# A hybrid attention and recurrent step: the recurrent unit's last tiles and the projections behind them in another order

## The chip, the cores and the metric

One core of a Trainium2 chip. The metric is the device time of one execution in microseconds (us), the median over runs of the same kernel. The engines are TensorE (PE, with its weight loads PEld), VectorE (DVE), ScalarE (ACT), GpSimd (POOL) and SyncE (SP, which here only issues DMAs).

## What is computed

Two layers of a hybrid trunk on 640 tokens (512 latent, 128 prompt) with 1024 features. Layer 0 mixes tokens by attention, layer 1 by a bidirectional gated linear recurrent unit; each is followed by a SwiGLU feed-forward network. The part around the change is the end of the attention and the recurrent unit with its output projection:

```python
def _lru_mixer(xm, h0, w_in, conv_w, conv_b, w_a, b_a, w_i, b_i, lam, w_out):
    gate, xr = jnp.split(xm @ w_in, 2, axis=-1)
    xc = _centred_depthwise_conv(xr, conv_w, conv_b).astype(jnp.float32)
    a_f, b_f = _rglru_coeffs(xc, w_a[0], b_a[0], w_i[0], b_i[0], lam[0])
    a_b, b_b = _rglru_coeffs(xc, w_a[1], b_a[1], w_i[1], b_i[1], lam[1])
    hs_f, hT_f = _linear_scan(a_f, b_f, h0[:, 0], reverse=False)
    hs_b, hT_b = _linear_scan(a_b, b_b, h0[:, 1], reverse=True)
    y = (hs_f + hs_b).astype(xm.dtype) * jax.nn.gelu(gate)
    return y @ w_out, jnp.stack([hT_f, hT_b], axis=1)
```

`_rglru_coeffs` holds two sigmoids, an exponential and a square root for each direction.

## The kernel before

Activations lie transposed: features on the 128 partitions, in 8 tiles of 128 features (k or f = 0..7), tokens in the free dimension. All matrix products run in a 32-bit format with the inputs split in two: a high part that is the cast of the value, and a low part that is the value minus the high part. `split` (L1331) makes both, the cast on ACT (L1333) and the subtraction on DVE (L1335). For each k a product takes three matmuls (`some`, L227 to L229): high weights by high input, high weights by low input, low weights by high input, all into one PSUM buffer. Groups of a unit of 128 output features cover the 640 tokens in two halves of 320 (in the recurrent unit 384 and 256).

The weights of such a unit are loaded by `unit`: the raw tile by SP, and the high part either by a cast on ACT (L180) or, in the recurrent unit, by a DMA that POOL issues (L178); the low part is DVE's (L182). High and low tiles have three buffers each in the names `whi` and `wlo`; a slot "x" has tiles of its own, `whx` and `wlx`. Plain PSUM groups have the name `mm` with three buffers; in the last stage three more are named `mx`.

The order of the instructions is set by a scheduler that plays the program through on a timeline, so code that moves shifts other work as well. `pin` makes one instruction wait for another in that order.

Attention works through 8 head pairs p. For the next pair, `qk` casts Q and K into high parts (QS, KS, on ACT) and subtracts for the low ones (KZ for K, on DVE), for two heads a = 0, 1. The call for pair 7 is made inside pair 6. Behind it, the attention's output O of pairs 0 to 6 is split into `ohi` and `olo`, pinned behind the K operations (`parted`), since the output projection of k=0..6 fills PE between the softmax steps of pair 7. Softmax goes by blocks: scores `sp` (L831, L832), operations on DVE and ACT into S, transposes `tp` (L849), and products with V `op` (L932). Pair 7's O is split last.

The recurrent unit runs over t, with tile f of each step one later than that of the step ahead: projection `lru_xr`, gate matmuls and tanh `lru_a` (L1291, L1292), coefficients `lru_b` (exponentials L1303, L1304; a square root L1305; two operations on DVE, L1306 and L1307), scans `lru_c` (L1316, the sums of both directions L1323 and L1324), the GELU branch `lru_gate` and the product `lru_d` (L1328) with the split of y into `yhi` and `ylo`. ACT holds one function table at a time, and `turn` (L1266) loads another (L1270) when a function of another table is due: exponentials with tanh, square root, gelu. `lru_gate` copies the first 384 tokens of a gate from PSUM (L1343) and takes the gelu of the last 256 straight from PSUM (L1346), which keeps that PSUM buffer until the table is there.

The projection behind it (`project_halves`) has 8 output units. Five groups start early, while y is not yet complete: units 0 and 1 in both halves and unit 2 in the first half. They go through k=0..5 group by group, then through k=6 and 7 group by group, each with its three matmuls per k; in between stand some matmuls that compute nothing needed (`keep`, L206). Then follow the other units, whose k all exist.

Of the kernel before, what the change touches and what calls it, by code (L numbers as in the profile page):

```python
# [125 lines left out]
class _Step:  # L126
# [33 lines left out]
        return self.t([P, KT, NTOK + 2], dt, "big", 4)[:, :, 0:n]  # L160


    def unit(self, src, slot=None, after=None):
        nc = self.nc
        _, a, b = src.shape
        raw = self.t([P, a, b], F32, "raw", 3)
        nc.sync.dma_start(raw, src)
        if slot is None:
            self.nu += 1
            slot = "x" if self.wx and self.nu % 2 == 0 else "m"  # L170
        if slot == "x":
            hi = self.t([P, a, b], F32R, "whx", 3, self.sb)
            lo = self.t([P, a, b], F32R, "wlx", 3, self.sb)
        else:
            hi = self.t([P, a, b], F32R, "whi", 3)
            lo = self.t([P, a, b], F32R, "wlo", 3)
        if self.ptags == ["at"]:
            nc.gpsimd.dma_start(hi, src)  # L178
        else:
            nc.scalar.copy(hi, raw)  # L180
        with self.tc.issue_after(after) if after else nullcontext():
            nc.vector.tensor_tensor(lo, raw, hi.bitcast(F32), ALU.subtract)  # L182
        return hi, lo
# [601 lines left out]
                nc.vector.tensor_copy(K[:, 832:960], ps[:, 192:320])  # L785
        return K, ek

    def qk(self, p, hi, lo, ap, Q=None, K=None):
# [12 lines left out]
        pairs = [(QS, Q, [Q, Q]), (KS, K, [KZ[:, 0], KZ[:, 1]])]  # L801
        for S, v, lo in pairs if p else pairs[::-1]:
            for a in range(2):
                hp = slice(a * HD, a * HD + HD)
                op = slice(HD - a * HD, P - a * HD)
                cast = nc.scalar.copy(S[hp, a], v[hp]).ins
                low = nc.vector.tensor_tensor(lo[a][hp], v[hp], S[hp, a].bitcast(F32), ALU.subtract).ins
                queue = nc.gpsimd if p in (0, 7) else nc.sync
                queue.dma_start(S[op, a].bitcast(F32), Q[hp] if v is Q else S[hp, a].bitcast(F32))
        self.parted = low, cast  # L810
        return QS, KS, KZ

    def vq(self, q, hi, lo, V):
# [214 lines left out]
    def project_halves(self, w, hi, lo, gk, key, xd):  # L1028
        def out(f, t0, t1, ps):
            self.residual(f, t0, t1, ps, G, True)  # L1030
            self.nc.sync.dma_start(xd[f * P:f * P + P, t0:t1], self.x[:, f, t0:t1])
        G = self.need(self.gcols, gk)
        us = [self.unit(w[f], "m") for f in range(3)]
        early = [(f, t0, t1) for f in range(3) for c, (t0, t1) in enumerate(CH) if c == 0 or f < KT - DEH]
        pss = [(self.ps("mx") if j % 2 else self.pg(False))[:, 0:HT] for j in range(len(early))]
        for ks in (range(KT - 2), range(KT - 2, KT)):
            if ks[0]:
                self.keep(self.ps("at"), 4)
            for (f, t0, t1), ps in zip(early, pss):
                self.some(us[f], hi, lo, t0, t1, ps, ks)  # L1040
                if ks[0]:
                    out(f, t0, t1, ps)
        for f in range(3, KT):
            us.append(self.unit(w[f], "mx"[f % 2]))
            out(f, *CH[0], self.chunk(us[f], hi, lo, *CH[0]))
        self.rt = self.t([P, NTOK], F32, "r", 2)
        for c, (t0, t1) in enumerate(CH):
            for f in range(KT - DEH, KT) if c else ():
                out(f, t0, t1, self.chunk(us[f], hi, lo, t0, t1))
                j = f - KT + DEH  # L1050
                for k in range(max(0, 2 * j - 2), 2 * j) if f < KT - 1 else ():
# [195 lines left out]
        c = CI["ba0"] * KT  # L1247
        nc.vector.tensor_scalar(self.hb, self.cols[:, c:c + 4 * KT], 0.5, None, ALU.mult)

    def halves(self, w, hi, lo, ev, after=None):  # L1250
        u = self.unit(w, None, after)
        return [lambda t0=t0, t1=t1, **kw: ev(t0, self.chunk(u, hi, lo, t0, t1, **kw)) for t0, t1 in CHL]

    def lru_xr(self, f, hi, lo, after=None):
# [70 lines left out]
        return y  # L1325

    def lru_d(self, f, y, G, yhi, ylo):
        self.nc.vector.tensor_tensor(y, y, G, ALU.mult)  # L1328
        self.split(yhi[:, f], ylo[:, f], y)

    def split(self, hi, lo, v, after=(None, None)):  # L1331
        with self.pin(after[1]):
# [4 lines left out]
    def lru_gate(self, f, hi, lo, lp, after=None):  # L1337
        nc = self.nc
        G = self.t([P, NTOK], F32, "gl", 3, lp)

        def ev(t0, ps):
            if t0 == 0:
                nc.scalar.copy(G[:, 0:384], ps)  # L1343
                return
            for v, o in ((ps, G[:, t0:NTOK]), (G[:, 0:t0], G[:, 0:t0])):
                self.turn(AF.Gelu_apprx_tanh, lambda: nc.scalar.activation(o, v, AF.Gelu_apprx_tanh))  # L1346
        return G, self.halves(self.i["wi"][f], hi, lo, ev, after)

    def new_x(self, st):
        pool = st.enter_context(self.tc.tile_pool(name="x", bufs=1, reuse_waits="tile"))  # L1350
# [6 lines left out]
    def run(self):  # L1357
# [35 lines left out]
        with self.phase("attn", tp=2, sp=2, op=1, quota=24) as ap:  # L1393
# [10 lines left out]
            for p in range(8):  # L1404
                if p == 3:
                    with self.pin(self.anchor):
                        self.lru_prep(ap)
                new = []
                self.attend(p, *QK, V, O, ap, (lambda: new.extend(self.qk(7, xhi, xlo, ap))) if p == 6 else None)
                if p == 5:  # L1410
                    self.need(self.AB, (0, 1, 1))
                if p < 7:
                    QK = new or self.qk(p + 1, xhi, xlo, ap, None if p else Q1)
                    if p % 2 == 1:
                        self.vq((p + 1) // 2, xhi, xlo, V)
                if p == 6:
                    ohi = self.big()
                    olo = self.big()
                    for k in range(KT - 1):
# [22 lines left out]
        with self.phase("lru", at=1) as lp:  # L1442
# [15 lines left out]
            for t in range(KT + 2):  # L1458
# [6 lines left out]
                    B[t - 1] = self.lru_b(t - 1, *A.pop(t - 1))  # L1465
                if t > 1:
                    C[t - 2] = self.lru_c(t - 2, *B.pop(t - 2))
                if t > 2:
                    for step in gate(t - 2):
                        step()  # L1470
                if t > 1:
                    self.lru_d(t - 2, C.pop(t - 2), G.pop(t - 2), yhi, ylo)
# [35 lines left out]
```

## Time and profile before

| what | before |
|---|---|
| time, median of 3 runs | 1517.01 us (1516.26 to 1520.28) |
| time of the profiled execution | 1518.63 us |
| its span in the profile | 1516.9 us |
| mean granted clock of TensorE | 0.996 |
| PE busy | 1490.0 us (98%) |
| DVE busy | 1063.5 us (70%) |
| ACT busy | 702.6 us (46%) |
| POOL busy | 260.6 us (17%) |

A row of a timeline gives the start, the duration of one instruction (or the length of a run of equal ones, xcount), the engine, the line, the operation, output and inputs, and in brackets the idle time of the engine just before it with the instruction that ended it. Matmuls overlap, so their rate is read from the distances of the starts. A row of the windows gives for each engine the busy time, then the granted clock, the share of the DMA engines and GB/s.

### The profile page before, as it was taken

How to read it: one execution, taken by the hardware profiler on the slowest of the kernel's cores; microseconds unless marked ns; L12 is line 12 of the kernel's file. 1: busy time of each engine (PE TensorE's matmuls, PEld its weight loads, DVE VectorE, ACT ScalarE, POOL GpSimd, SP SyncE). 2: the span in 40 equal slices, each digit the busy share in tenths (PEclk: the TensorE clock that was granted, in tenths of full speed). 3: DMA queues.
4: the chain of work that ended last, by engine and by line, in shares of the span. 5: the costliest groups of instructions: out<-in, count | busy, mean ns of one | idle time of the engine just before them, and what ended most of it. 6: DMA issues, size and time to landing. Idle time of an engine off the chain costs nothing. (4 is left out here: it accounts for less than half of the span.)

```text
span 1516.9 us, 26173 instructions
## 1 busy us (share of the span) xinstructions
PE 1490.0 (98%) x10397; PEld 1443.2 (95%) x10397; DVE 1063.5 (70%) x2005; ACT 702.6 (46%) x1270; POOL 260.6 (17%) x276
## 2 busy tenths in 40 slices
PE   8999999999999999999999999989999999999997
PEld 6999999899999999999999988889999999999997
DVE  5778998679999997434443768886975665566555
ACT  4676766654332123312321568884644342434243
POOL 0112132101111110000000014230332323222211
PEclk9999999999999999999999999999999999999999
DMA  9544665446566664222222544325242231323211
GB/s 376 175 142 159 187 190 168 118 141 193 180 182 196 206 197 132 62 84 84 65 69 87 153 133 128 105 68 198 70 152 84 70 112 56 104 64 98 70 57 70
DMA packets 72330, 196.65 MB, mean 130 GB/s; under 512 B 8048, under 2 KB 24592, under 8 KB 72080
## 3 DMA queue, kind: packets, MB, share of 16 engines
q1 hardware_dynamic: 57392, 142.32, 29.7%
q0 software_dynamic: 14240, 51.98, 11.3%
q8 instruction: 81, 1.33, 0.4%
q10 hardware_dynamic: 576, 0.68, 0.1%
q14 instruction: 41, 0.34, 0.1%
HBM read 179.48 MB, written 8.92 MB: 124 GB/s over the span
## 5 line engine op out<-in xcount | busy, mean ns | idle before, releaser
L227 PE MATMUL mm<-big,whi 128*128 128x320 f32 (+3 forms) x1233 | 385.4, 314 | 5.7 <-ACT gl L1346 3.0
L228 PE MATMUL mm<-big,whi 128*128 128x320 f32 (+3 forms) x1233 | 384.8, 312 | 4.9 <-DVE big L1335 4.7
L229 PE MATMUL mm<-big,wlo 128*128 128x320 f32 (+3 forms) x1233 | 383.5, 312 | 0.0
L227 PEld LDWEIGHTS mm<-big,whi 128*128 128x128 f32 x1233 | 233.7, 190 | 8.6 <-ACT gl L1346 3.5
L228 PEld LDWEIGHTS mm<-big,whi 128*128 128x128 f32 x1233 | 234.1, 190 | 6.9 <-DVE big L1335 5.3
L229 PEld LDWEIGHTS mm<-big,wlo 128*128 128x128 f32 x1233 | 233.6, 190 | 1.0
L256 DVE SCALAR_TENSOR_TENSOR mprod<-mraw,csb 128x1024 f32<-128x1024 f32 x160 | 195.6, 1222 | 11.9 <-DMA mraw<-in_wm 11.4
L597 DVE SCALAR_TENSOR_TENSOR x<-mm,G,x 128x320 f32<-128x320 f32 (+2 forms) x192 | 78.0, 435 | 81.8 <-PE mm L229 81.5
L180 ACT CAST whi<-raw 128x1024 fp32r<-128x1024 f32 (+1 forms) x71 | 73.9, 1041 | 112.5 <-PE mm L228 65.5
L182 DVE TENSOR_TENSOR wlo<-raw,whi 128x1024 fp32r<-128x1024 f32 (+1 forms) x87 | 105.8, 1216 | 27.4 <-ACT whi L180 11.4
L227 PE MATMUL mm<-big,whx 128*128 128x320 f32 (+3 forms) x348 | 108.3, 311 | 0.0
L229 PE MATMUL mm<-big,wlx 128*128 128x320 f32 (+3 forms) x348 | 108.0, 310 | 0.0
L228 PE MATMUL mm<-big,whx 128*128 128x320 f32 (+3 forms) x348 | 107.8, 310 | 0.0
L252 POOL DMA_DIRECT2D mraw<-in_wm x80 | 43.1, 539 | 359.0 <-DVE mprod L256 266.1
L227 PE MATMUL mx<-big,whi 128*128 128x320 f32 (+3 forms) x287 | 89.1, 311 | 0.0
L229 PE MATMUL mx<-big,wlo 128*128 128x320 f32 (+3 forms) x287 | 88.8, 310 | 0.0
L228 PE MATMUL mx<-big,whi 128*128 128x320 f32 (+3 forms) x287 | 88.6, 309 | 0.0
L180 ACT CAST whx<-raw 128x1024 fp32r<-128x1024 f32 (+1 forms) x40 | 41.1, 1030 | 86.7 <-PE mm L228 47.6
L227 PE MATMUL mx<-big,whx 128*128 128x320 f32 (+3 forms) x260 | 80.6, 310 | 0.0
L229 PE MATMUL mx<-big,wlx 128*128 128x320 f32 (+3 forms) x260 | 80.5, 310 | 0.0
L228 PE MATMUL mx<-big,whx 128*128 128x320 f32 (+3 forms) x260 | 80.3, 309 | 0.0
L1333 ACT CAST whi<-raw 128x1024 fp32r<-128x1024 f32 (+1 forms) x41 | 41.3, 1008 | 70.8 <-PE mm L228 44.8
(349 smaller groups left out, 3727.8 us busy)
## 6 DMA issues: line engine op xcount, KB each, us to landing
raw<-in_gu SPq DMA_DIRECT2D x88, 512.0 KB, 3.5
mraw<-in_wm POOLq DMA_DIRECT2D x80, 512.0 KB, 4.0
raw<-in_dn SPq DMA_DIRECT2D x24, 512.0 KB, 3.6
sw<-in_wm SPq DMA_DIRECT2D x16, 512.0 KB, 10.5
raw<-in_wqk SPq DMA_DIRECT2D x16, 512.0 KB, 4.6
raw<-in_wi SPq DMA_DIRECT2D x16, 512.0 KB, 3.5
whi<-in_wi POOLq DMA_DIRECT2D x16, 512.0 KB, 4.0
raw<-in_dn SPq DMA_DIRECT2D x16, 448.0 KB, 3.3
```

Of the source, the lines that this page charges most:

```text
L180: nc.scalar.copy(hi, raw)
L182: nc.vector.tensor_tensor(lo, raw, hi.bitcast(F32), ALU.subtract)
L227: nc.tensor.matmul(ps, hi[:, k], xhi[:, k, s], start=(k == 0), stop=False)
L228: nc.tensor.matmul(ps, hi[:, k], xlo[:, k, s], start=False, stop=False)
L229: self.done = nc.tensor.matmul(ps, lo[:, k], xhi[:, k, s], start=False, stop=(k == last)).ins
L252: nc.gpsimd.dma_start(w, self.i["wm"][l * 6 + j - 2, f])
L256: nc.vector.scalar_tensor_tensor(prod, w, 1.0, self.csb[:, s], ALU.mult, ALU.mult, accum_out=out[:, s, f:f + 1])
L597: self.nc.vector.scalar_tensor_tensor(xs, ps[:, a - t0:b - t0], G[:, s, f:f + 1], xs, ALU.mult, ALU.add)
L1333: self.nc.scalar.copy(hi, v)
```

## The change

Four things change.

1. `project_halves`: the five early groups go through k=0..4 group by group. Then k=5, 6 and 7 have a pass each: within a pass, over all five groups sorted by token half, first both matmuls with the high input (high and low weights), then for all groups the one with the low input. The keep-alive matmuls stand ahead of k=7 only.
2. The recurrent unit's last tiles: gates 5 and 6 have their gelus in one step (t=7), under one load of the table, and gate 7 comes a step earlier (t=8). Gate 7's second half is copied from PSUM like the first, and one gelu of 640 works in place. For tile 7 the product and the split go in two halves of 320.
3. The weights of gates 6 and 7 go into `whx` and `wlx`, two buffers each, so `whi` and `wlo` are free sooner for the projection's first units.
4. At the end of attention, the split of O[0] is issued between the K casts of pair 7: the cast (L815 after) behind the first K cast, the low part (L817 after) behind the first KZ operation.

```diff
-    def unit(self, src, slot=None, after=None):
+    def unit(self, src, slot=None, after=None, nx=3):
...
-            hi = self.t([P, a, b], F32R, "whx", 3, self.sb)
-            lo = self.t([P, a, b], F32R, "wlx", 3, self.sb)
+            hi = self.t([P, a, b], F32R, "whx", nx, self.sb)
+            lo = self.t([P, a, b], F32R, "wlx", nx, self.sb)
...
-                cast = nc.scalar.copy(S[hp, a], v[hp]).ins
+                with self.pin(self.opened if a and S is KS and p == 7 else None):
+                    cast = nc.scalar.copy(S[hp, a], v[hp]).ins
...
-        self.parted = low, cast
+                self.parted = low, cast
+                if p == 7 and S is KS and a == 0:
+                    ohi, olo = self.outs = self.big(), self.big()
+                    with self.pin(cast):
+                        self.opened = nc.scalar.copy(ohi[:, 0], O[:, 0]).ins
+                    with self.pin(low):
+                        nc.vector.tensor_tensor(olo[:, 0], O[:, 0], ohi[:, 0].bitcast(F32), ALU.subtract)
...
-        for ks in (range(KT - 2), range(KT - 2, KT)):
-            if ks[0]:
+        for (f, t0, t1), ps in zip(early, pss):
+            self.some(us[f], hi, lo, t0, t1, ps, range(KT - 3))
+        turns = sorted(zip(early, pss), key=lambda e: e[0][1])
+        for k in range(KT - 3, KT):
+            if k == KT - 1:
                 self.keep(self.ps("at"), 4)
-            for (f, t0, t1), ps in zip(early, pss):
-                self.some(us[f], hi, lo, t0, t1, ps, ks)
-                if ks[0]:
+            for (f, t0, t1), ps in turns:
+                for part in us[f]:
+                    self.done = self.nc.tensor.matmul(ps, part[:, k], hi[:, k, t0:t1], start=False, stop=False).ins
+            for (f, t0, t1), ps in turns:
+                self.done = self.nc.tensor.matmul(ps, us[f][0][:, k], lo[:, k, t0:t1], start=False, stop=(k == KT - 1)).ins
+                if k == KT - 1:
                     out(f, t0, t1, ps)
...
-    def halves(self, w, hi, lo, ev, after=None):
-        u = self.unit(w, None, after)
+    def halves(self, w, hi, lo, ev, after=None, slot=None):
+        u = self.unit(w, slot, after, 2)
...
-        self.nc.vector.tensor_tensor(y, y, G, ALU.mult)
-        self.split(yhi[:, f], ylo[:, f], y)
+        for a, b in CH if f == KT - 1 else ((0, NTOK),):
+            self.nc.vector.tensor_tensor(y[:, a:b], y[:, a:b], G[:, a:b], ALU.mult)
+            self.split(yhi[:, f, a:b], ylo[:, f, a:b], y[:, a:b])
...
+            if t0 == 0 or f == KT - 1:
+                nc.scalar.copy(G[:, t0:t0 + ps.shape[1]], ps)
             if t0 == 0:
-                nc.scalar.copy(G[:, 0:384], ps)
                 return
-            for v, o in ((ps, G[:, t0:NTOK]), (G[:, 0:t0], G[:, 0:t0])):
+            for v, o in ((G, G),) if f == KT - 1 else ((ps, G[:, t0:NTOK]), (G[:, 0:t0], G[:, 0:t0])):
                 self.turn(AF.Gelu_apprx_tanh, lambda: nc.scalar.activation(o, v, AF.Gelu_apprx_tanh))
-        return G, self.halves(self.i["wi"][f], hi, lo, ev, after)
+        return G, self.halves(self.i["wi"][f], hi, lo, ev, after, "x" if f > KT - 3 else None)
...
-                if t > 2:
-                    for step in gate(t - 2):
+                for g in {KT - 1: (KT - 3, KT - 2), KT: (KT - 1,)}.get(t, (t - 2,)):
+                    for step in gate(g) if 0 < g < KT - 1 + (t == KT) else ():
                         step()
```

The line numbers of after are higher: the split's L1333 and L1335 are L1347 and L1349, the gelu L1346 is L1361, the copy L1343 is L1357, the square root L1305 is L1318, the table load L1270 is L1283.

The order on ACT at the end of the recurrent unit, before: from the exponentials of tile 7 (`lt_1733`) through the square root and the two gelus to the casts of y6 (`lt_1739`) and y7 (`lt_1746`); `gl_1747` is gate 6 and `gl_1753` gate 7.

```order
L1270 ACT_TABLE_LOAD
L1305 ACTIVATE lt_1733_10624<-lt_1733_10624 128x1286
L1270 ACT_TABLE_LOAD
L1346 ACTIVATE gl_1747_10747<-mm_1752_10780 128x256
L1346 ACTIVATE gl_1747_10747<-gl_1747_10747 128x384
L1346 ACTIVATE gl_1753_10820<-mm_1758_10853 128x256
L1346 ACTIVATE gl_1753_10820<-gl_1753_10820 128x384
L1333 CAST big_1595_9509<-lt_1739_10644 128x640
L1333 CAST big_1595_9509<-lt_1746_10727 128x640
```

The same place on ACT after, where `gl_1746` is gate 6, `gl_1753` gate 7, `lt_1724` y5, `lt_1739` y6 and `lt_1752` y7; the gelu of gate 5 stands just ahead of the first row.

```order
L1361 ACTIVATE gl_1746_10724<-mm_1751_10757 128x256
L1361 ACTIVATE gl_1746_10724<-gl_1746_10724 128x384
L1283 ACT_TABLE_LOAD
L1316 ACTIVATE lt_1752_10787<-lt_1733_10624,l_sm4_387_2014 128x643
L1357 COPY gl_1753_10807<-mm_1758_10840 128x256
L1347 CAST big_1595_9509<-lt_1724_10534 128x640
L1317 ACTIVATE lt_1733_10624<-lt_1733_10624,l_sp2_386_2012 128x643
L1316 ACTIVATE lt_1752_10787<-lt_1733_10624,l_sm4_387_2014 128x643
L1317 ACTIVATE lt_1733_10624<-lt_1733_10624,l_sp2_386_2012 128x643
L1283 ACT_TABLE_LOAD
L1347 CAST big_1595_9509<-lt_1739_10644 128x640
L1318 ACTIVATE lt_1733_10624<-lt_1733_10624 128x1286
```

Gelu 6, the copy of gate 7's second half and the cast of y6 have moved ahead of the square root of tile 7; behind it are left one gelu and the two half casts of y7.

The order on PE from the keep-alive matmuls (`at`) on, before: `big_1595` is the high y, `big_1596` the low y, and `mm` and `mx` are the early groups.

```order
L210 MATMUL at_1777_11016<-ident_2_63,ones_5_72 128x128 x4
L227 MATMUL mm_1772_10921<-big_1595_9509,whi_1764_10905 128x320
L228 MATMUL mm_1772_10921<-big_1596_9510,whi_1764_10905 128x320
L229 MATMUL mm_1772_10921<-big_1595_9509,wlo_1765_10909 128x320
L227 MATMUL mx_1773_10922<-big_1595_9509,whi_1764_10905 128x320
L228 MATMUL mx_1773_10922<-big_1596_9510,whi_1764_10905 128x320
L229 MATMUL mx_1773_10922<-big_1595_9509,wlo_1765_10909 128x320
```

On PE after, the end of the pass of k=6 (its last two low-input matmuls), the keep-alive matmuls and the start of the pass of k=7:

```order
L1053 MATMUL mx_1773_10925<-big_1596_9510,whi_1764_10908 128x320
L1053 MATMUL mx_1775_10927<-big_1596_9510,whi_1767_10914 128x320
L210 MATMUL at_1777_11034<-ident_2_63,ones_5_72 128x128 x4
L1051 MATMUL mm_1772_10924<-big_1595_9509,whi_1764_10908 128x320
L1051 MATMUL mm_1772_10924<-big_1595_9509,wlo_1765_10909 128x320
L1051 MATMUL mm_1774_10926<-big_1595_9509,whi_1767_10914 128x320
L1051 MATMUL mm_1774_10926<-big_1595_9509,wlo_1768_10915 128x320
L1051 MATMUL mm_1776_10928<-big_1595_9509,whi_1770_10920 128x320
L1051 MATMUL mm_1776_10928<-big_1595_9509,wlo_1771_10921 128x320
```

Before, 30 matmuls of k=6 and 7 stand behind the keep-alive ones, and the third group (`mm_1776`) does k=0..5 just ahead of them; after, 15 of k=7 stand there, and k=6 stands ahead.

The order on DVE at the end of attention, before, from the second KZ operation of pair 7 on; `big_787` is the low O, `big_786` its high part.

```order
L807 TENSOR_TENSOR KZ1_80_576<-K_742_3660,KS_749_3724 64x960
L868 TENSOR_REDUCE mx_779_3810<-sp_782_3813 128x1
L1335 TENSOR_TENSOR big_787_3855<-big_78_568,big_786_3854 128x640 x2
L868 TENSOR_REDUCE mx_779_3810<-sp_783_3817 128x1
L1335 TENSOR_TENSOR big_787_3855<-big_78_568,big_786_3854 128x640 x3
```

The same place after, where `big_751` is the low O:

```order
L817 TENSOR_TENSOR big_751_3735<-big_78_568,big_750_3734 128x640
L875 TENSOR_REDUCE mx_781_3814<-sp_784_3817 128x1
L808 TENSOR_TENSOR KZ1_80_576<-K_742_3660,KS_749_3724 64x960
L1349 TENSOR_TENSOR big_751_3735<-big_78_568,big_750_3734 128x640
L875 TENSOR_REDUCE mx_781_3814<-sp_785_3821 128x1
L1349 TENSOR_TENSOR big_751_3735<-big_78_568,big_750_3734 128x640 x3
```

The low part of O[0] has moved ahead of the second KZ operation; that of O[1] stands behind it as before.

More of the change, by code (lines that the diff above doesn't have):

```diff
@@ L786, in keys_tile, with qk @@
         return K, ek
-    def qk(self, p, hi, lo, ap, Q=None, K=None):
+    def qk(self, p, hi, lo, ap, Q=None, K=None, O=None):
         nc = self.nc
@@ L1408, in run @@
                 new = []
-                self.attend(p, *QK, V, O, ap, (lambda: new.extend(self.qk(7, xhi, xlo, ap))) if p == 6 else None)
+                self.attend(p, *QK, V, O, ap, (lambda: new.extend(self.qk(7, xhi, xlo, ap, None, None, O))) if p == 6 else None)
                 if p == 5:
@@ L1416, in run @@
                 if p == 6:
-                    ohi = self.big()
-                    olo = self.big()
-                    for k in range(KT - 1):
+                    ohi, olo = self.outs
+                    for k in range(1, KT - 1):
                         self.split(ohi[:, k], olo[:, k], O[:, k], self.parted)
```

## The prediction

> **What bounds the kernel now.** I read the page first, then the list of waits for TensorE, then the busy time of each engine by stretch, and last the timelines of PE, ACT and DVE around the two places that the change touches.
>
> ```profile
> span 1516.9 us, 26173 instructions
> PE 1490.0 (98%) x10397; PEld 1443.2 (95%) x10397; DVE 1063.5 (70%) x2005; ACT 702.6 (46%) x1270; POOL 260.6 (17%) x276
> ```
>
> TensorE is busy for 1490.0 of 1516.9 us, so all its idle time together is 26.9 us, and an edit that leaves the number of matmuls alone can only win from that rest and from stretches in which the clock is low. The edit leaves it alone. The list of waits (line, releaser, total, times, longest) says where the rest is:
>
> ```profile
> PE mm L228 <- DVE big L1335: 4.7, 2, 3.4
> PE mm L227 <- ACT gl L1346: 3.0, 2, 1.7
> PE mm L227 <- ACT big L1333: 1.7, 3, 0.8
> ```
>
> These three are exactly the things that the change works on: low parts of a late input (L1335), a gelu that still holds a PSUM buffer (L1346), and high parts of a late input (L1333). In two stretches, the end of the recurrent unit and the end of attention (length, then PE, PEld, DVE, ACT, POOL busy, clock, DMA share, GB/s):
>
> ```profile
> 300.00:330.00 30.00, 28.87 (x258) 26.46 (x257) 18.75 (x59) 17.82 (x44) 1.09 (x2) 1.00 0.33 124
> ...
> 1000.00:1020.00 20.00, 14.56 (x84) 13.77 (x83) 18.46 (x24) 13.57 (x19) 7.45 (x5) 0.83 0.10 28
> ```
>
> From 1000 to 1020 PE lacks 5.4 us, at a granted clock of 0.83, while DVE is busy for 18.46 of 20: there the elementwise chain on DVE and ACT sets the end. The PE timeline shows the two holes and what follows them:
>
> ```profile
> 1004.80 0.41 PE L227 MATMUL mm<-big,whi 128*128 128x320 f32 x1 [0.41 <-ACT big L1333]
> ...
> 1008.87 0.42 PE L228 MATMUL mm<-big,whi 128*128 128x320 f32 x1 [3.37 <-DVE big L1335]
> ...
> 1011.69 0.64 PE L227 MATMUL mm<-big,whi 128*128 128x320 f32 x1 [1.67 <-ACT gl L1346]
> ...
> 1016.39 0.47 PE L229 MATMUL mm<-big,wlo 128*128 128x320 f32 x1
> 1016.65 0.35 PE L227 MATMUL mm<-big,whi 128*128 128x320 f32 x1
> 1016.84 0.31 PE L228 MATMUL mm<-big,whi 128*128 128x320 f32 x1
> 1016.99 0.31 PE L229 MATMUL mm<-big,wlo 128*128 128x320 f32 x1
> ...
> 1019.37 1.05 PE L210 MATMUL at<-ident,ones 128*128 128x128 f32 x8
> 1020.18 0.39 PE L227 MATMUL mm<-big,whi 128*128 128x320 f32 x1
> ...
> 1024.72 0.31 PE L227 MATMUL mx<-big,whx 128*128 128x320 f32 x1
> ```
>
> A 320-wide matmul starts every 0.15 us at full clock (1016.84 to 1016.99) and every 0.26 us at half (1016.39 to 1016.65). Half clock lasts from 1011.69 to 1016.65, 4.96 us, which costs 4.96 x (1 - 0.149/0.267) = 2.2 us. The second pass (k=6,7, 30 matmuls) begins at 1020.18, and the next unit, which needs nothing late, at 1024.72: that is the mark by which I measure this place.
>
> **The end of the recurrent unit.** First ACT and DVE, the chain to y7:
>
> ```profile
> 1003.09 1.04 ACT L180 CAST whi<-raw 128x1024 fp32r<-128x1024 f32 x1
> 1004.03 0.72 ACT L1333 CAST big<-lt 128x640 fp32r<-128x640 f32 x1
> ...
> 1008.66 1.28 ACT L1305 ACTIVATE lt<-lt 128x1286 f32<-128x1286 f32 x1
> ...
> 1011.95 0.38 ACT L1346 ACTIVATE gl<-mm 128x256 f32<-128x256 f32 x1
> 1012.21 0.52 ACT L1346 ACTIVATE gl<-gl 128x384 f32<-128x384 f32 x1
> ...
> 1019.76 0.73 ACT L1333 CAST big<-lt 128x640 fp32r<-128x640 f32 x1 [5.26 <-DVE lt L1328]
> ```
>
> ```profile
> 1009.97 1.50 DVE L1306 SCALAR_TENSOR_TENSOR lt<-lt,lt 128x1286 f32<-128x1286 f32 x1 [1.16 <-ACT lt L1305]
> 1011.51 1.50 DVE L1307 TENSOR_TENSOR lt<-lt,lt 128x1286 f32<-128x1286 f32 x1
> 1012.92 0.82 DVE L1328 TENSOR_TENSOR lt<-lt,gl 128x640 f32<-128x640 f32 x1
> 1013.66 1.28 DVE L1316 TENSOR_TENSOR_SCAN lt<-lt,cols,lt 128x512 f32<-128x512 f32 x1
> ...
> 1016.66 0.80 DVE L1335 TENSOR_TENSOR big<-lt,big 128x640 fp32r<-128x640 f32 x1
> 1017.38 1.29 DVE L1323 TENSOR_TENSOR lt<-lt 128x64 f32<-128x64 f32 x2
> ...
> 1018.90 0.83 DVE L1328 TENSOR_TENSOR lt<-lt,gl 128x640 f32<-128x640 f32 x1
> 1020.52 0.83 DVE L1335 TENSOR_TENSOR big<-lt,big 128x640 fp32r<-128x640 f32 x1 [0.79 <-ACT big L1333]
> ```
>
> In the chain to y7 ACT's square root (1008.66, ended 1009.94) starts DVE. Ahead of it on ACT, by the new order, one weight cast goes (1003.09 to the next start 1004.03: -0.94), gelu 6 comes (1011.95 and 1012.21: +0.8), the copy of gate 7's second half comes (no row of that form; between 0 and the 0.39 of a gelu of the same shape, and nearest to that: +0.35) and the cast of y6 comes (0.72, some 0.65 start to start). The number of table loads is the same. Sum +0.85: the square root ends at about 1010.8.
>
> On DVE two things leave the chain: the product of y6 (1012.92 to 1013.66, 0.74) and its low part (1016.66 to 1017.38, 0.72). Both now run while DVE waits for that square root. So: 1010.8, plus 2.95 for the two long operations, plus 3.0 for the scans (1013.66 to 1016.66), plus 1.52 for the sums (1017.38 to 1018.90) is 1018.3. The product is cut in two halves of some 0.45 each (between half of 0.83 and the whole), and the cast likewise: the first half's high part is there at about 1019.2. Before, PE began with it at 1020.18. The tail of this chain is a gain of 1.0.
>
> What does PE do until then? Before, of the 20.3 us from 1004.39 (0.41 ahead of 1004.80) to 1024.72, 5.45 were waits (0.41, 3.37, 1.67), 2.2 half clock and 0.8 the keep-alive matmuls (1019.37 to 1020.18); 11.9 is work, 2.2 of it (15 x 0.149) the k=7 matmuls. If neither y5, y6 nor a gelu stops it, PE is through with k=0..6 at 1004.4 + 9.7 = 1014.1. Gelu 6 and both high parts stand on ACT, and both low parts on DVE, ahead of tile 7's square root at 1010.8, and PE comes to y6 only with its last 15 matmuls before 1014.1; so I see nothing that stops it. PE then runs the keep-alive matmuls and idles for some 4 us, in one piece. The waits of 3.37 and 1.67 are not abolished, they become this one; what is won is that only 15 matmuls stand behind it and not 30. With full clock: 1019.2 + 2.25 = 1021.5, a gain of 3.2. With half clock: in before the clock fell after holes of 3.37 and 1.67, so 4 us of idleness should bring it down too. Its price is between that of the shorter stretch of half clock below (3.1 us, so 1.4) and 2.2: end at 1022.9 to 1023.7, a gain of 1.0 to 1.8. I take 1.4, the middle.
>
> A side cost: two of the weight casts (1.04 each) now stand ahead of gelu 4 on ACT, which frees the PSUM buffer of gate 6's second half. PE may stop there for 0 to 2.1 us. That is inside the later 4 us of idleness, except for what reaches tile 7's gate matmuls and so ACT: I take 0.2. Sum here: **-1.2 us**.
>
> The cover of the weights: their DMAs for gates 6 and 7 stand first in POOL's queue now, ahead of the unit below, whose low part waited for its landing.
>
> ```profile
> 864.25 0.57 POOL L178 DMA_DIRECT2D whi<-in_wi  x1 [13.96 <-PE mm L229]
> ```
>
> ```profile
> 868.15 1.22 DVE L182 TENSOR_TENSOR wlo<-raw,whi 128x1024 fp32r<-128x1024 f32 x1 [0.70 <-DMA whi<-in_wi]
> ```
>
> From issue to use are 3.9 us. POOL sits idle for 13.96 us before it, so issuing costs nothing; the second new load waits for DVE's last norm operation and may overlap the old one for a while. I take 0; the bounds are 0 and 3.9, if the whole old load queues behind the new one. A gain there has no place, since PE does not wait.
>
> **The end of attention.** ACT, DVE and PE:
>
> ```profile
> 289.72 0.72 ACT L1333 CAST big<-big 128x640 fp32r<-128x640 f32 x1
> ```
>
> ```profile
> 290.87 1.16 DVE L807 TENSOR_TENSOR KZ<-K,KS 64x960 fp32r<-64x960 f32 x1
> ...
> 292.38 1.56 DVE L1335 TENSOR_TENSOR big<-big,big 128x640 fp32r<-128x640 f32 x2
> ```
>
> ```profile
> 290.50 0.70 PE L227 MATMUL mm<-big,whi 128*128 128x320 f32 x3 [0.83 <-ACT big L1333]
> ...
> 293.26 0.64 PE L228 MATMUL mm<-big,whi 128*128 128x320 f32 x1 [1.31 <-DVE big L1335]
> ...
> 296.36 0.40 PE L227 MATMUL mm<-big,whi 128*128 128x320 f32 x1
> ...
> 299.68 0.39 PE L831 MATMUL sp<-KS,QS 128*128 128x512 f32 x1
> ```
>
> The cast of O[0] goes up by one K cast (about 1.0) and its low part ahead of the second KZ operation (1.16). The wait of 1.31 for O[0]'s low part goes. What is late next is the low part of k=1, still behind that KZ operation: 290.87 + 0.78 (half of 1.56) + 1.16 + 0.78 = 293.6, where k=0's ended at 293.16. PE has k=0's remaining matmuls and the scores to do in between and comes there some 0.65 before (an estimate, between 0 and 1.31). The 0.83 remains in another form, since the transposes wait for an S that ACT scales behind the same casts as before; I take 1.0 for it, between 0.83 and the 1.31 of the other wait. Waits go from 2.14 to 1.65, a gain of 0.5. Half clock from 293.26 to 296.36 (3.1 us) costs 1.4 now; if it goes, the gain is 1.9. Against it: 12 filler matmuls (1.8 us) more now stand ahead of the first scores of head pair 7 (299.68), and fewer between its softmaxes, where PE lacks 1.13 of 30 us already. That can take back up to 1.3. Bounds -1.9 and +0.8; I take **-0.6**, nearest to the case in which the clock falls as it did.
>
> **The sum.** -1.2 and -0.6 are -1.8 us: the profiled execution's 1518.63 us (its span is 1516.9) becomes 1516.8. That execution lies 1.6 above the median of 1517.01, so I forecast a median of **1515.2 us**. 0.3% are 4.55 us, about what a measurement of this kernel tells from no change: faster means below 1512.5, slower above 1521.6.
>
> **Rivals.**
>
> *The clock stays full at both places* (0.15). For it: neither hole in front of 1011.69 brought it down at once, since the matmuls from 1008.87 ran at 0.15 us; against it, both places have half clock now. Gains of 3.2 and 1.9: 1511.9 us, faster. The Trainium skill ("TensorE: Matmul & The Clock Gate", Part 1: The HAM clock gate) has the clock fall after at least one free-running idle window of about 3.4 us; by that rule one hole of 4 us holds a whole window only in some of the runs, and this rival would be the likelier. The trace speaks against so mild a rule: the clock was down at 1011.69 after holes of 3.37 and 1.67, neither of 3.4.
>
> *Nothing is left* (0.19). Softmax of pair 7 takes the attention gain back (0), and the k=7 pass starts later by 0.6 and at the full 2.2 of half clock (gain 0.4, no more): 1516.6 to 1517.4, the same. For it: the chain is DVE's, and DVE is at 18.46 of 20.
>
> *The new loads delay the old ones* (0.06). If DMAs are served in order, the unit issued at 864.25 lands 3.9 us later, PE stops at the start of the recurrent unit, and the clock falls for another 2.2: 6.1 lost against 1.8 won is +4.3, so 1521.3; with no gain at the other end 1523.1. It decides from the point where that load lands after about 869. Against it: POOL's idle 13.96 us ahead of it.
>
> The forecast has the remaining 0.60, with 1513.6 to 1516.8 of its own. Faster: 0.13 of the first rival and 0.01 of the forecast's tail, 0.14. Slower: 0.05 of the third. Same: 0.81. The range from 1511.5 to 1518.5 leaves out the third rival and the ends of the first two.
>
> **What would show it.** Right: no wait for a gelu or for L1349 before k=7; one hole of some 4 us, ending near 1019 on before's scale; half clock behind it; the next unit 1.0 to 1.8 us sooner. In attention a wait of about 0.65 in place of 1.31. Wrong: a hole before k=5 or 6, a y7 chain that begins after 1011.5, full clock in the k=7 pass, or a stop of PE near 869.

## The result and the profile after

The changed kernel took 1523.72 us, the median of 7 runs (1522.17 to 1525.52), against 1520.28 us (7 runs, 1516.26 to 1522.2) for the kernel before in the same series. The ratio is 1.0029, with a 95% interval of 1.0019 to 1.0038. So it is slower, by about 4 us; I had forecast 1515.2 us and a gain of 1.8. Of the 8.5 us between forecast and measured time, 3.3 lie in the starting point: the median of 1517.01 that I started from, of three runs, is 1520.28 in seven. The profiled execution took 1523.53 us with a span of 1520.6.

The list of waits for TensorE after, to be held against the three rows of before:

```profile
PE mm L1051 <- ACT big L1347: 4.1, 1, 4.1
PE mm L227 <- ACT gl L1361: 3.0, 2, 2.2
PE gp L1304 <- DVE xc L1294: 2.5, 1, 2.5
...
PE tp L856 <- ACT S L851: 1.0, 1, 1.0
...
PE mm L228 <- DVE big L1349: 0.6, 1, 0.6
```

The first row is the one hole ahead of k=7 that I expected. The third is new and stands in none of my cases: PE waits for the conv output xc in the middle of the recurrent unit.

To see where the time went I use marks on PE at which both kernels have done the same matmuls. First before: the transposes that stand ahead of the work on pair 7's K, the first matmul behind attention, the norm ahead of the recurrent unit, tile 7's gate matmuls, the wait for the first product of the second feed-forward stage, and a wait near the end (the next unit, at 1024.72, is quoted in the prediction).

```profile
288.62 0.66 PE L849 MATMUL tp<-ident,S 128*128 128x128 f32 x4 [0.18 <-DVE S L846]
...
321.82 0.42 PE L227 MATMUL mx<-big,whi 128*128 128x320 f32 x1
...
846.46 0.49 PE L550 MATMUL at<-ones,ssq 128*128 128x128 f32 x2 [0.67 <-DVE ssq L536]
...
988.37 2.33 PE L1291 MATMUL gp<-xc,gw 128*128 128x512 f32 x8
...
1104.78 0.41 PE L1154 MATMUL mm<-xt,whx 128*128 128x320 f32 x1 [1.39 <-DVE g L1116]
...
1484.25 0.45 PE L227 MATMUL mm<-big,whi 128*128 128x384 f32 x1 [0.42 <-ACT big L1333]
```

The PE timeline after, the same marks and what lies between:

```profile
288.44 0.66 PE L856 MATMUL tp<-ident,S 128*128 128x128 f32 x4 [0.18 <-DVE S L853]
...
320.11 0.42 PE L227 MATMUL mx<-big,whi 128*128 128x320 f32 x1
...
844.73 0.49 PE L550 MATMUL at<-ones,ssq 128*128 128x128 f32 x2 [0.64 <-DVE ssq L536]
...
932.02 0.44 PE L227 MATMUL mm<-big,whi 128*128 128x384 f32 x1 [2.20 <-ACT gl L1361]
...
932.91 0.53 PE L228 MATMUL mm<-big,whi 128*128 128x384 f32 x1
933.23 0.53 PE L229 MATMUL mm<-big,wlo 128*128 128x384 f32 x1
...
968.22 2.43 PE L1304 MATMUL gp<-xc,gw 128*128 128x512 f32 x8 [2.51 <-DVE xc L1294]
...
989.93 0.38 PE L227 MATMUL mm<-big,whx 128*128 128x256 f32 x1 [0.83 <-ACT gl L1361]
...
992.90 2.33 PE L1304 MATMUL gp<-xc,gw 128*128 128x512 f32 x8
...
1022.77 0.63 PE L1051 MATMUL mm<-big,whi 128*128 128x320 f32 x1 [4.06 <-ACT big L1347]
...
1026.94 0.47 PE L227 MATMUL mx<-big,whx 128*128 128x320 f32 x1
...
1028.27 0.32 PE L229 MATMUL mx<-big,wlx 128*128 128x320 f32 x1
...
1107.86 0.42 PE L1167 MATMUL mm<-xt,whx 128*128 128x320 f32 x1 [1.75 <-DVE g L1129]
...
1488.01 0.45 PE L227 MATMUL mm<-big,whi 128*128 128x384 f32 x1 [0.42 <-ACT big L1347]
```

The differences of the marks give each stretch; every row is one profiled execution. "Start" is the time up to the first mark, where no kernel differs from another; that it still goes from 288.1 to 290.8 shows the scatter of a single execution. "Attention" goes to the second mark. From there to the norm all take 524.5 to 524.7 us. "Body" goes from the norm to tile 7's gate matmuls, "end" from there to the next unit, "next" from there to the first product, "rest" from there to the last mark. The kernels other than before and after are those of the experiments below.

| profile | start | attention | body | end | next | rest |
|---|---|---|---|---|---|---|
| before | 288.62 | 33.20 | 141.91 | 36.35 | 80.06 | 379.47 |
| after | 288.44 | 31.67 | 148.17 | 34.04 | 80.92 | 380.15 |
| `x_only` | 290.83 | 33.26 | 151.31 | 34.45 | 80.31 | 381.31 |
| `no_attn` | 288.39 | 33.15 | 150.95 | 33.58 | 80.10 | 379.51 |
| `attn_only` | 288.81 | 31.67 | 141.72 | 35.74 | 79.84 | 379.34 |
| `all_but_x` | 288.60 | 31.65 | 141.85 | 35.74 | 80.38 | 379.40 |
| `x_low_late` | 288.51 | 31.97 | 145.43 | 33.91 | 79.83 | 379.35 |
| `x_st_dve` | 288.51 | 34.40 | 142.78 | 33.91 | 79.79 | 379.11 |
| `after_low_late` | 288.68 | 31.68 | 145.91 | 34.02 | 81.01 | 379.15 |
| `after_st_dve` | 288.12 | 31.68 | 142.73 | 34.13 | 80.73 | 379.53 |
| `after_late_x` | 288.63 | 31.68 | 142.91 | 33.71 | 80.22 | 379.15 |
| `keep_28` | 288.60 | 31.68 | 141.89 | 33.92 | 82.38 | 379.50 |
| `after_late_keep` | 288.60 | 31.67 | 143.04 | 32.34 | 81.01 | 379.28 |

From before to after: -0.2 at the start, -1.5 at attention, +6.3 in the body of the recurrent unit, -2.3 at its end, +0.9 and +0.7 behind: +3.8. The two places that I worked out did better than I had said; a place that I had priced at nothing lost 6.3 us.

In that place, the POOL timeline before. Each row is a load of a unit's high weights, or the copy of one column, the last state of a tile's scan.

```profile
920.35 0.76 POOL L178 DMA_DIRECT2D whi<-in_wi  x1 [6.51 <-PE mm L229]
922.62 1.02 POOL L1318 COPY st<-lt 128x1 f32<-128x1 f32 x1 [1.52 <-DVE lt L1316]
924.11 3.87 POOL L1318 COPY st<-lt 128x1 f32<-128x1 f32 x1 [0.47 <-DVE lt L1316]
```

And after:

```profile
921.70 1.02 POOL L1331 COPY st<-lt 128x1 f32<-128x1 f32 x1 [9.89 <-ACT xr L1276]
923.19 2.69 POOL L1331 COPY st<-lt 128x1 f32<-128x1 f32 x1 [0.47 <-DVE lt L1329]
925.83 0.53 POOL L178 DMA_DIRECT2D whi<-in_wi  x1
```

The load of gate 3's weights stood ahead of the copies of tile 1 and now stands behind them. It is issued 5.5 us later and no longer waits for PE to free its buffer: POOL waits for tile 1's scans and then takes 2.69 us for one column. From its issue to its landing the load takes 3.7 us. What this does on DVE, before (weights' low parts L182, conv operations L1281, first operation behind the square root L1306):

```profile
926.66 1.27 DVE L182 TENSOR_TENSOR wlo<-raw,whi 128x1024 fp32r<-128x1024 f32 x1
927.80 2.79 DVE L1281 SCALAR_TENSOR_TENSOR xc<-xr,cols,xc 128x643 f32<-128x643 f32 x3
...
947.48 1.22 DVE L182 TENSOR_TENSOR wlo<-raw,whi 128x1024 fp32r<-128x1024 f32 x1 [4.10 <-issue]
948.62 1.49 DVE L1306 SCALAR_TENSOR_TENSOR lt<-lt,lt 128x1286 f32<-128x1286 f32 x1
```

And after:

```profile
929.63 1.23 DVE L182 TENSOR_TENSOR wlo<-raw,whi 128x1024 fp32r<-128x1024 f32 x1 [3.80 <-issue]
930.77 2.73 DVE L1294 SCALAR_TENSOR_TENSOR xc<-xr,cols,xc 128x643 f32<-128x643 f32 x3
...
945.75 1.23 DVE L182 TENSOR_TENSOR wlx<-raw,whx 128x1024 fp32r<-128x1024 f32 x1
951.46 1.22 DVE L182 TENSOR_TENSOR wlx<-raw,whx 128x1024 fp32r<-128x1024 f32 x1 [4.49 <-DMA raw<-in_wi]
952.61 1.49 DVE L1319 SCALAR_TENSOR_TENSOR lt<-lt,lt 128x1286 f32<-128x1286 f32 x1
```

DVE works in order, so the conv operations behind the late load's low part start at 930.77 and not 927.80. Some 20 us on, two more low parts (of gates 6 and 7, which PE uses some 40 us later: the row at 989.93 is gate 6's second half) stand ahead of L1319, the second of them waiting for a raw tile: L1319 starts at 952.61 and not 948.62. With the 1.7 us by which the norm came sooner, DVE is 5.7 us late there. Then PE stops for xc. A wait of this kind is not new: the 4.10 us before, ahead of 947.48, is for a load that POOL issued only at 943.66, behind a copy of one column of 5.32 us and once PE had freed the buffer.

My theory from this: the third part of the change (the buffers of their own) does it, by two delays of DVE: **(B)** gate 3's load behind a POOL copy, **(C)** the early low parts of gates 6 and 7. Rivals: attention's lead only meets a gelu that comes no earlier, and the clock falls; or the new order of the gelus delays ACT.

### The profile page after: what moved, and what is told of

It reads as the page before. It is cut to its first block, busy times and chain, and to the rows that moved or that the text cites. A ratio compares the mean times of both kernels' runs of the same rounds, so it can differ in the third digit from the quotient of the medians.

```text
span 1520.6 us, 26172 instructions
## 1 busy us (share of the span) xinstructions
PE 1492.0 (98%) x10397; PEld 1444.1 (95%) x10397; DVE 1064.4 (70%) x2007; ACT 702.9 (46%) x1271; POOL 268.3 (18%) x276
## 5 line engine op out<-in xcount | busy, mean ns | idle before, releaser
L227 PE MATMUL mm<-big,whi 128*128 128x320 f32 (+3 forms) x1192 | 371.0, 313 | 3.6 <-ACT gl L1361 2.2
L228 PE MATMUL mm<-big,whi 128*128 128x320 f32 (+3 forms) x1192 | 371.1, 312 | 0.8 <-DVE big L1349 0.6
L229 PE MATMUL mm<-big,wlo 128*128 128x320 f32 (+3 forms) x1192 | 370.1, 311 | 0.0
L227 PEld LDWEIGHTS mm<-big,whi 128*128 128x128 f32 x1192 | 224.8, 189 | 5.9 <-ACT gl L1361 2.4
L228 PEld LDWEIGHTS mm<-big,whi 128*128 128x128 f32 x1192 | 225.4, 189 | 2.6 <-DVE big L1349 0.8
L229 PEld LDWEIGHTS mm<-big,wlo 128*128 128x128 f32 x1192 | 225.0, 189 | 1.1
L227 PE MATMUL mm<-big,whx 128*128 128x320 f32 (+3 forms) x380 | 118.5, 312 | 0.8 <-ACT gl L1361 0.8
L182 DVE TENSOR_TENSOR wlo<-raw,whi 128x1024 fp32r<-128x1024 f32 (+1 forms) x85 | 103.2, 1214 | 22.5 <-ACT whi L180 13.1
L229 PE MATMUL mm<-big,wlx 128*128 128x320 f32 (+3 forms) x380 | 117.8, 310 | 0.0
L228 PE MATMUL mm<-big,whx 128*128 128x320 f32 (+3 forms) x380 | 117.7, 310 | 0.0
L227 PE MATMUL mx<-big,whi 128*128 128x320 f32 (+3 forms) x281 | 87.4, 311 | 0.0
L228 PE MATMUL mx<-big,whi 128*128 128x320 f32 (+3 forms) x281 | 86.8, 309 | 0.0
L1347 ACT CAST whi<-raw 128x1024 fp32r<-128x1024 f32 (+1 forms) x41 | 41.4, 1009 | 72.5 <-PE mm L228 45.1
```

The costliest lines, as they stand in the source:

```text
L227: nc.tensor.matmul(ps, hi[:, k], xhi[:, k, s], start=(k == 0), stop=False)
L228: nc.tensor.matmul(ps, hi[:, k], xlo[:, k, s], start=False, stop=False)
L229: self.done = nc.tensor.matmul(ps, lo[:, k], xhi[:, k, s], start=False, stop=(k == last)).ins
L1347: self.nc.scalar.copy(hi, v)
```

## The experiments

The parts of the change are called A (attention), P (the passes of the projection), G (gates, gelus, the halves of tile 7) and X (the buffers of their own). Each ratio is to the kernel before.

**X alone.** The edit to the kernel before, which leaves A, P and G out:

```diff
-        return G, self.halves(self.i["wi"][f], hi, lo, ev, after)
+        return G, self.halves(self.i["wi"][f], hi, lo, ev, after, "x" if f > KT - 3 else None)
```

> The kernel before with the third part of the change alone: gates 6 and 7 take their weights in buffers of their own. Theory (the new loads stand first in POOL's queue, so that a copy of a scan's last state, which waits for DVE, now stands ahead of the load of tile 5's weights, and DVE then waits for that load in front of tile 2's conv operations; and the low parts of gates 6 and 7 come early and make DVE wait for a raw tile): slower by 3 to 6 us, with a DVE wait of 3 to 4 us ahead of a weight's low part near 930 us and a PE wait for xc near 968. Rival 1 (the lead of the attention part runs into a gelu that comes no earlier, and the clock falls): no change within 1 us. Rival 2 (the new order of the gelus delays ACT): no change within 1 us.

1522.88 us, ratio 1.0033 (1.0019 to 1.0048). The loss is there with X alone: 4.2 us by the medians (1518.67 before in that series), 5.0 by the ratio. Its profiled execution took 1530.78 us, some 8 above its median, so its row in the table shows more than the usual loss. (The expectation says tile 5's weights and tile 2's conv; the rows are gate 3's weights and tile 5's conv.)

**All but X.** The changed kernel with that line undone.

> The changed kernel with its third part undone: gates 6 and 7 take weights from the common buffers. Theory: faster than before by 2 to 4 us (attention 1.7 to 1.9, the recurrent unit's end 1 to 2, less what gelu 1 takes back). Rival 1 (attention's lead and the clock): slower by 1 to 3 us. Rival 2 (order of the gelus): slower by 1 to 3 us.

1517.1 us, ratio 0.9988 (0.9979 to 0.9997): 1.8 us faster, a little under what was expected. The body of the recurrent unit is back at 141.85. Both rivals fall: A and G are in this kernel, and nothing is lost.

**A alone.** The kernel before with the split of O[0] between the K casts, without P, G and X.

> The kernel before with the attention part alone. Theory: faster by 0.5 to 1.8 us; the lead of 1.7 us at the end of attention is kept but for a longer wait for gelu 1 (up to 0.9). Rival 1: the wait for gelu 1 grows from 1.4 to about 2.2 us and the clock falls to half behind it for some 3 us, so that nothing is left: within 0.5 us of before or slower by up to 1 us. Rival 2: faster by 1.7 us.

1516.42 us, ratio 0.9992 (0.9982 to 1.0002). By the interval it may be nothing; in the profile attention takes 31.67 and not 33.20, the wait for gelu 1 shrinks to 1.17 us in place of growing, and nothing behind takes longer.

**All but A.** The changed kernel with attention as before.

> The changed kernel with the attention part undone. Theory: slower than before by 3 to 6 us, so as slow as the changed kernel or 1 to 2 us slower. Rival 1: no slower than before within 1 us. Rival 2: slower by 4 to 6 us.

1525.58 us, ratio 1.0043 (1.0029 to 1.0058). By the ratios, 1.0043 against 1.0029, A is worth about 2 us in the changed kernel; the intervals overlap, so the size is not sure. Its profile has the stop for xc at its plainest, with the clock at half behind it (4.66 us for the eight gate matmuls that took 2.33 before):

```profile
969.51 4.66 PE L1297 MATMUL gp<-xc,gw 128*128 128x512 f32 x8 [3.94 <-DVE xc L1287]
```

**B alone.** X, with the low parts of gates 6 and 7 pinned late:

```diff
-                G[g], halves = self.lru_gate(g, xhi, xlo, lp, after)
+                G[g], halves = self.lru_gate(g, xhi, xlo, lp, self.convs[g] if g > KT - 3 else after)
```

(`convs[f]` is the last conv operation of tile f.)

> The kernel before with the third part alone, and the low parts of gates 6 and 7 on DVE pinned behind the conv operations of tiles 6 and 7, about where they stood before. POOL's order stays the one of the third part: the load of gate 3's weights behind the copy of tile 1's last states. If that copy on POOL is the cause: slower than before by 2 to 5 us, with the DVE wait of 3 to 4 us ahead of gate 3's low part. If the early low parts of gates 6 and 7 (waiting for a raw tile) are the cause: no slower than before within 1 us.

1519.37 us, ratio 1.0000 (0.9992 to 1.0009). The DVE wait is there,

```profile
930.17 1.22 DVE L182 TENSOR_TENSOR wlo<-raw,whi 128x1024 fp32r<-128x1024 f32 x1 [3.89 <-PE mm L228]
```

but PE does not stop for xc. Read with the table, B is not free: the body takes 3.5 us more than before, the end 2.4 less. Of the 3.5, 0.9 is a longer wait for gelu 1 (2.28 and not 1.37), 0.8 a wait at gelu 4 that every kernel with X has, and about 1.5 half clock behind the first of the two (matmuls 0.32 us apart and not 0.17, for 3.4 us).

**C alone.** X, with the copies of the states on DVE:

```diff
-            nc.gpsimd.tensor_copy(st, h[:, d, e:e + 1])
+            nc.vector.tensor_copy(st, h[:, d, e:e + 1])
```

> The kernel before with the third part alone, and the copies of the scans' last states on DVE and not on POOL, so that no load stands behind one; the low parts of gates 6 and 7 stay early. 16 one-column operations more on DVE (some 0.1 us each by the one-column reciprocals of the attention, 1 to 2 us of DVE in all). If the POOL copy is the cause: within 1 us of before, or slower by up to 2 us for the DVE operations and the early low parts. If the early low parts are the cause: slower by 3 to 5 us, with a DVE wait of over 4 us for a raw tile near 951.

1519.06 us, ratio 0.9999 (0.999 to 1.0008). The second early low part waits as long as before the edit, and the first delay is gone:

```profile
927.93 1.23 DVE L182 TENSOR_TENSOR wlo<-raw,whi 128x1024 fp32r<-128x1024 f32 x1 [0.61 <-issue]
...
949.23 1.23 DVE L182 TENSOR_TENSOR wlx<-raw,whx 128x1024 fp32r<-128x1024 f32 x1 [3.98 <-DMA raw<-in_wi]
```

So X costs 4 to 5 us with both delays and nothing that can be measured with either. My expectation that B would show by itself as 2 to 5 us was wrong, and so was the simple sum. One thing is left untested: this edit takes all 16 copies off POOL, and what that is worth without X was not run.

**Both early places undone in the changed kernel.** A, P, G and X, with POOL's loads of gates 6 and 7 pinned behind the copy of tile 3's states, where they stood before:

```diff
-            nc.gpsimd.dma_start(hi, src)
+            with self.pin(self.sts[3] if slot == "x" else None):
+                nc.gpsimd.dma_start(hi, src)
```

(`sts[3]` is that copy.)

> The changed kernel, whole, with one edit: POOL's loads of gates 6 and 7 are pinned behind the copy of tile 3's last states, where they stood before. Theory: all of the loss goes; faster than before by 2 to 4 us, as the changed kernel without the third part or up to 1 us better, since the weight casts of the projection stay early on ACT. Rival (it is the buffers themselves or the new places of the casts on ACT): slower than before by 2 us or more.

1516.23 us, ratio 0.9987 (0.9978 to 0.9996). All of the loss goes with one pin. The buffers are not at fault, only where the scheduler put the loads. It is no better than all but X by more than the noise.

**Each delay alone in the changed kernel.** The same edits as for C and B, on the changed kernel.

> The changed kernel with one edit: the copies of the scans' last states run on DVE, so that no load stands behind a POOL copy; the early low parts of gates 6 and 7 stay. If the two delays of DVE are harmless one at a time and stop PE only together: faster than before by 1 to 2.5 us, no PE wait for xc. If the early low parts do harm by themselves once attention is ahead: slower than before by 1 us or more.

1517.3 us, ratio 0.9993 (0.9984 to 1.0001).

> The changed kernel with one edit: the low parts of gates 6 and 7 pinned behind the conv operations of tiles 6 and 7; POOL's order stays. If the two delays are harmless one at a time: faster than before by 0.5 to 2.5 us, the wait for gelu 1 stays at 2.2 us or more, but there is no PE wait for xc. If the POOL copy does harm by itself once attention is ahead (the wait for gelu 1 and the clock): slower than before by up to 2 us.

1517.74 us, ratio 0.9996 (0.9986 to 1.0005). Its profile has a short stop for xc (0.98 us) and a wait for gelu 1 of 2.47 us. In the table the body takes 142.73 with C alone, 142.91 with neither, 145.91 with B alone and 148.17 with both. So in these profiles, with A, P and G about, C adds nothing by itself, B some 3.0 us, and C on top of B another 2.3. Each is one execution, and that of B alone took 1520.59 us, 2.9 above its median. The times say less of B: 0.9996 with it and 0.9987 with neither are 1.4 us, and the intervals overlap. What the times do show is that either delay alone leaves the kernel at or a little below the time of before, and both together bring the loss.

**The clock behind the hole.** All but X, with 28 keep-alive matmuls ahead of k=7:

```diff
-                self.keep(self.ps("at"), 4)
+                self.keep(self.ps("at"), 28)
```

> The changed kernel without its third part, with 28 keep-alive matmuls ahead of the k=7 pass in place of 4 (24 more, some 4.8 us by the 0.8 us of the 4), which fill the 5.4 us hole. If half clock behind that hole costs what I took (1.4 to 2.2 us): the k=7 pass runs at full clock, and the time is 1.2 to 2.2 us below the kernel with 4. If the keep-alive matmuls reach past the arrival of y7: as much later as they reach, up to 0.5 us.

1516.39 us, ratio 0.9986 (0.9978 to 0.9995), against 0.9988 with 4. The PE timeline with 4 keep-alive matmuls:

```profile
1018.19 0.64 PE L1051 MATMUL mm<-big,whi 128*128 128x320 f32 x1 [5.39 <-ACT big L1347]
1018.62 0.47 PE L1051 MATMUL mm<-big,wlo 128*128 128x320 f32 x1
1018.89 0.47 PE L1051 MATMUL mm<-big,whi 128*128 128x320 f32 x1
```

With 28:

```profile
1011.95 6.41 PE L210 MATMUL at<-ident,ones 128*128 128x128 f32 x56
1018.39 0.41 PE L1051 MATMUL mm<-big,whi 128*128 128x320 f32 x1
1018.64 0.31 PE L1051 MATMUL mm<-big,wlo 128*128 128x320 f32 x1
1018.79 0.31 PE L1051 MATMUL mm<-big,whi 128*128 128x320 f32 x1
```

With 28 the pass begins 0.2 us later and runs at 0.15 us a matmul and not 0.27: the end of the unit takes 33.92 and not 35.74, a gain of 1.8, inside my 1.4 to 2.2. But the time does not show it. The next stretch takes 82.38 and not 80.38: PE now waits there for a weight's cast and low part (0.29 and 0.69) and longer for the first product (1.97 and not 1.36), 1.6 us of the 2.0.

**The best of it.** The changed kernel with the late loads and 24 keep-alive matmuls.

> The changed kernel with POOL's loads of gates 6 and 7 pinned late and 24 keep-alive matmuls ahead of the k=7 pass in place of 4 (20 more, some 4.3 us by the 6.41 us of 28, against a hole of 4.05). From the two edits apart: the mark of the next unit 1 us earlier than with the late loads alone; of it about half or less in the time, since in the kernel with 28 the next stage gave most of it back in waits for weights and for the first products of its DVE. So faster than before by 2 to 3.5 us.

1515.06 us, ratio 0.9979 (0.997 to 0.9989): about 3.2 us faster than before, and the fastest here. The end takes 32.34, 1.4 less than with the late loads alone (33.71), of which the next stretch gives back 0.8 (81.01 and not 80.22).

## Why the prediction was wrong

**The step that failed** is "The cover of the weights". I wrote that issuing the two new loads costs nothing since POOL is idle ahead of the load at 864.25, and took 0 with bounds of 0 and 3.9. I priced the load that stands next to the new ones and not the rest of the queue. Moving two loads to its head also turned the order of a load and two copies about 60 us later, and of two low parts on DVE some 80 us later; both changes can be read in the order of the two programs, and I had not followed them. Waits in front of instructions that are due stop everything behind them on an in-order engine. The runs put 4 to 5 us on this part by itself (`x_only`), where the prediction had 0, and `after_late_x` takes the loss away by putting those two loads back.

**The third rival** had the right part and the wrong place. It feared that the load at 864.25 would come later; PE shows no wait from there on until gelu 1, near 932.

**Attention**: I took -0.6. It was -1.5, nearer to the 1.9 of the case in which the clock stays up. The waits came out as worked, 0.97 and 0.55 for about 1.0 and 0.65,

```profile
290.94 0.66 PE L856 MATMUL tp<-ident,S 128*128 128x128 f32 x4 [0.97 <-ACT S L851]
...
293.70 0.42 PE L228 MATMUL mm<-big,whi 128*128 128x320 f32 x1 [0.55 <-DVE big L1349]
293.96 0.31 PE L229 MATMUL mm<-big,wlo 128*128 128x320 f32 x1
294.11 0.31 PE L227 MATMUL mm<-big,whi 128*128 128x320 f32 x1
```

but the matmuls run at full clock here, in all eight profiles with A (31.65 to 31.68 us); of five without A four had half clock (33.15 to 34.40) and one did not (31.97). The mis-sized term is the clock.

**The recurrent unit's end**: the hole is in one piece and 4.06 us long, as said ("some 4 us"). The chain on ACT and DVE was right: from the end of the square root to the first half's cast I had 8.0 us (9.8 before); the rows give 1022.26 - 1014.34 = 7.9.

```profile
1013.06 1.28 ACT L1318 ACTIVATE lt<-lt 128x1286 f32<-128x1286 f32 x1
...
1022.26 0.86 ACT L1347 CAST big<-lt 128x320 fp32r<-128x320 f32 x2 [5.87 <-DVE lt L1342]
```

Half clock came, from 1022.77 to about 1028.27: 5.5 us, a price of 2.4 where I had 1.4 to 2.2; the last 1.3 us of it lie behind the mark, in "next". From tile 7's gate matmuls the end gained 2.3. But this depends on X: without it the weight cast stays on ACT ahead of the square root (the 0.94 of my sum), and `all_but_x` takes 35.74, as `attn_only` does with none of P and G. And X without P and G has the short end too (33.91 in `x_low_late` and `x_st_dve`); body and end together take 176.69 us in `x_st_dve` and 176.86 in `after_st_dve`, which has P and G. So the 2.3 us are not owed to P and G, which show no gain of their own here with X or without. They show one only with more keep-alive matmuls, and those were not run in the old order.

**The side cost** at gelu 4 was 0.83 us, between my 0 and 2.1; it appears in every kernel with X, with the late pin too.

Without X the gain would have come out as forecast: -1.8, and -1.8 measured (-3.2 to -0.5 by the interval). That is partly luck, since the two terms were off in opposite ways: attention gave 1.5 and not 0.6, the end 0.6 and not 1.2, and that 0.6 is there without P and G as well.

What stays open: in the profile of C alone body and end together are 1.6 us shorter than before, and its median time is not (its attention took 1.2 longer in that one execution). And with B the wait for gelu 1 is longer, 1.67 to 2.47 us in five kernels, against 0.87 to 1.38 in the eight without; why, I have not tried.

## What to carry to other kernels

When a buffer of its own lets a load start sooner, read the whole queue that it moves up in, to the end of the stage, and on each in-order engine look for due instructions that now stand behind one that waits. Delays of this kind need not add up: each of two may fit under the slack, and both together stop the bound engine. The cure can be a pin that puts the early load back, rather than giving up the buffers.

## What the runs showed of the hardware

A POOL copy of one column can take very long while DVE is busy. Its durations after (smallest, median and largest in ns), and of the same 16 copies on DVE in `x_st_dve`:

```profile
L1331 POOL COPY st<-lt x16: 1003/1118/8894, 902.1 to 1020.7; 128x1 f32<-128x1 f32 x16
```

```profile
L1318 DVE COPY st<-lt x16: 132/146/207, 906.9 to 1018.8; 128x1 f32<-128x1 f32 x16
```

The Trainium skill ("SBUF — State Buffer", Who interferes with whom) says that a DVE instruction with two SBUF inputs contends with a GpSimd instruction that reads SBUF. The trace fits that, with 8.89 us for one column while DVE ran such operations. It also shows when the long copies end: before and after have seven copies of over 2 us each, and in each trace five of the seven end 0.04 to 0.06 us after DVE falls idle. The copy of 923.19 ends at 925.88, and DVE's run of operations had ended at 925.84. So a load that stands behind such a copy goes out about when DVE stops, and if DVE stops for that very load, it waits for about the whole transfer: 3.80 us after, with a transfer of 3.7, against 0.61 in `x_st_dve`, where no load stands behind a copy. That DVE holds the copy up is read from these ends; no run here isolates it.

The clock does not go by the length of a hole alone. Behind 2.20 us at the wait for gelu 1 (after) it fell to half within four matmuls (932.91 to 933.23 is 0.32 us, 0.17 at full clock), and behind 2.28 us (`x_low_late`) it fell 1.3 us after the hole; at the same place it did not behind 2.47 us (`after_low_late`), nor behind the 2.51 us for xc (after: 2.43 us for eight gate matmuls, 2.33 without a hole). Behind 4.06 and 5.39 us ahead of k=7 it did. The Trainium skill ("TensorE: Matmul & The Clock Gate", Part 1: The HAM clock gate) has a free-running window, which would make it depend on where a hole falls, and asks for an idle window of about 3.4 us; the falls behind 2.20 and 2.28 us do not agree with that length.
